# Two-layer encoder trunk on one core: rows of x and of the output moved one residue class per DMA, on two queues

## The chip, the cores and the metric

One core of one Trainium2 chip runs the whole program. The metric is device time in microseconds (us) of one execution, from the first to the last instruction. A program of this length is measured over several runs, and the median is compared.

## The reference, cut to what matters

```python
D_MODEL, SEQ, DEPTH, D_FF = 2048, 256, 2, 5632

def hybrid_layer(x, rel_bias, w_in, sink, w_pa, w_pb, w_out, ln1_g, ln1_b, w_up, w_down, ln2_g, ln2_b):
    proj = jnp.einsum('bsd,dc->bsc', x, w_in)                      # 10240 columns
    qa, ka, va, qb, kb, vb, ga, gb = jnp.split(proj, split_points, axis=-1)
    ya = dilated_mixture(qa, ka, va, rel_bias) @ w_pa              # dilations 1, 4, 16
    yb = windowed_gqa(qb, kb, vb, rel_bias, sink) @ w_pb
    merged = jax.nn.sigmoid(ga) * ya + jax.nn.sigmoid(gb) * yb
    x = layer_norm(DEEPNORM_ALPHA * x + merged @ w_out, ln1_g, ln1_b)
    gate, up = jnp.split(x @ w_up, 2, axis=-1)
    return layer_norm(DEEPNORM_ALPHA * x + (jax.nn.silu(gate) * up) @ w_down, ln2_g, ln2_b)

def reference(x, ...):                                             # x: (1, 256, 2048) float32
    for l in range(DEPTH):
        x = hybrid_layer(x, ...)
    return x
```

x and the output are 2.10 MB each (256 rows of 8 KB); the weights of both layers, all float32, are some 500 MB.

## The kernel before, in words

**Tokens.** The 256 tokens are kept in an order of residue classes: the rows 4q + a, q = 0 to 63, of class a (0 to 3) stand together. So a tile of 128 partitions holds two classes: half t = 0 has classes 0 and 1, half t = 1 classes 2 and 3. The residual stream lies in four tiles res[c] (c = 0 to 3), each [128 partitions, 2 halves, 512 columns]. token_rows (lines 70 to 73) describes in DRAM the rows of one half t: two classes of 64 rows each, 4 rows apart, 512 columns (2 KB) of each row. load_x(c) (lines 308 to 310) loads column chunk c of x by two DMAs, one for each half; leave (lines 786 to 789) multiplies, adds and stores one chunk of one half.

**Weights.** All products stream their weights in pieces of 512 KB (128 partitions of 1024 float32). load_to (line 118) issues a piece's DMA on SP's queue into one of six raw buffers; split_to makes two exact parts of it, the high one on ACT (line 128, whi) and the low one on DVE (line 129, wlo). Each product is three matmuls (lines 215 to 217 with the activations stationary, 171 and 202 with the weights stationary). run (lines 137 to 152) goes through the pieces in program order; splits are issued three pieces ahead of the products (fewer for the first two pieces), loads five further, as far as the six raw buffers are free. Every engine and every queue executes in the order in which the code issues.

**Start.** busy(n) issues n matmuls of zeros on PE (line 316). Then come the loads of x and of the first weights on SP, then make(0) and make(1). make(i) transposes two 128-column tiles of x with the identity on PE (line 369, four matmuls), copies the result as the high part on ACT (line 290) and takes the low part on DVE (line 291); the tile is called xT. make(2) to make(7) run just ahead of pieces 0 to 5 of the first product; chunk c of x serves make(2c) and make(2c + 1). Piece j of the first product needs tile xT j. The first product (group 0 of va) has 8 pieces of two row tiles of w_in, each with 12 matmuls of 512 columns (two row tiles, two halves of the tokens, three products); its result is taken off PSUM by ACT at line 290 (va<-acc). Ahead of piece 6 setup_small issues 15 small loads on SP (lines 324 to 335).

**Just after the start.** The bias table ftab is written to DRAM by 7 DMAs of 640 KB on SP (line 351), one after each of seven pieces, so these writes and weight loads take turns in SP's queue.

**End.** The last layer norm works on half t = 0, then on t = 1; for each, DVE alternates centre (line 784) and leave (line 788) over the four chunks, and SP issues a store after each leave (line 789).

Of the kernel before, what the change touches and what calls it, by code (L numbers as in the profile page):

```python
# [17 lines left out]
D_MODEL = 2048  # L18
SEQ = 256
# [27 lines left out]
def bias_tables():  # L47
    """Over the offsets key - query, in the order [residue difference][quotient difference]: one-hot rows
    (group, bucket), and what masks the offsets out of a head's reach; both depend on shapes alone."""
    half = NUM_BUCKETS // 2  # L50
    exact = half // 2
    delta = np.arange(-3, 4)[:, None]
    step = np.arange(-63, 65)[None, :]
    d = 4 * step + delta
    n = np.abs(d)
    scaled = np.log(np.maximum(n, 1) / exact) / math.log(MAX_DISTANCE / exact)
    large = np.minimum(exact + (scaled * (half - exact)).astype(np.int64), half - 1)
    bucket = np.where(d > 0, half, 0) + np.where(n < exact, n, large)
    keep = [(d % dil == 0) & (n <= (win // (2 * dil)) * dil) for win, dil in A_GROUPS]
    keep.append(n <= B_HALF)  # L60
    hot = np.zeros((4, NUM_BUCKETS, 7, P), np.float32)
    mask = np.zeros((N_HEADS, 7, P), np.float32)
    for g, ok in enumerate(keep):
        for b in range(NUM_BUCKETS):
            hot[g, b] = ok & (bucket == b)
        mask[A_HG * g:(A_HG * (g + 1) if g < 3 else N_HEADS)] = np.where(ok, 0.0, NEG)
    return hot.reshape(4 * NUM_BUCKETS, 7 * P), mask.reshape(N_HEADS, 7 * P)


def token_rows(dram, t, c0, width):  # L70
    """Rows of a (SEQ, D_MODEL) array in the kernel's order: position 64 * (i % 4) + i // 4."""
    return bass.AP(tensor=dram.tensor, offset=dram.offset + 2 * t * D_MODEL + c0,
                   ap=[[D_MODEL, 2], [4 * D_MODEL, 64], [1, width]])


@with_exitstack
def trunk(ctx: ExitStack, tc: tile.TileContext, x, rel_bias, w_in, sink, w_pa, w_pb, w_out,
          ln1_g, ln1_b, w_up, w_down, ln2_g, ln2_b, hot, mask, eye, out):
    nc = tc.nc
# [23 lines left out]

# [1 line left out]
    pieces = []  # L105
# [31 lines left out]
    def run():  # L137
        """Splits run ahead of the products, further ahead where a layer norm follows."""
        for m, pc in enumerate(pieces):
            ahead = min(AHEAD_SPLIT, 1 + m)  # L140
            for n in norms:
                if n - 24 <= m < n:
                    ahead = max(ahead, min(n - m + AHEAD_NORM, AHEAD_SPLIT + (m - n + 24) // 3))
            split_to(m + 1 + ahead)
            if pc["pre"]:
                pc["pre"]()
            pc["mm"](pc)
            if pc["post"]:
                pc["post"]()
            if background:  # L150
                background.pop(0)()
            pieces[m] = None
# [4 lines left out]
    def gemm_w(w, c0, xs, post, pre=None, turn=None):  # L157
        """out^T (256 columns of w from c0, tokens): weights stationary. With turn, the products with the
        high parts of the first half of the tokens come before turn(), which makes the second half."""
        kts = w.shape[0] // P  # L160
# [58 lines left out]
    def gemm_a(w, k0, k1, c0, width, xs, post, pre=None, turn=None):  # L219
        """out (tokens, width columns of w from c0) over the row tiles k0:k1: activations stationary. With  # L220
        turn, some products with the first half of the tokens come before turn(), which makes the second."""
        kk = 1024 // width
# [27 lines left out]
    def gemm_a_halves(w, k0, k1, c0, width, xs, post, between):  # L250
        """As gemm_a, with the first half of the tokens done before the second is begun."""
        kk = 1024 // width
# [40 lines left out]
    def triple(out, a, b, start, stop):  # L293
        """out (+)= a^T b by the parts (high, low) of both."""
        nc.tensor.matmul(out, lhsT=a[0], rhs=b[0], start=start, stop=False)  # L295
        nc.tensor.matmul(out, lhsT=a[0], rhs=b[1], start=False, stop=False)  # L296
        nc.tensor.matmul(out, lhsT=a[1], rhs=b[0], start=False, stop=stop)  # L297

# [1 line left out]
    res = [const.tile([P, 2, 512], F32, name=f"res{c}") for c in range(4)]  # L300
# [7 lines left out]
    def load_x(c):  # L308
        for t in range(2):
            nc.sync.dma_start(res[c][:, t, :], token_rows(x, t, c * 512, 512))  # L310

    def busy(n):
        """Keeps the tensor engine's clock up where it waits for operands."""
        ps = acc_tile()
        for _ in range(n):
            nc.tensor.matmul(ps[:, 0, 0:256], lhsT=zeros[:, 0:P], rhs=zeros, start=True, stop=True)
# [38 lines left out]
    def load_bias(dst, head, t, a0, na):  # L355
        """dst (128 queries of half t, na * 64 keys): bias by key - query, masked where out of reach."""
        for e in range(2):
# [4 lines left out]

# [1 line left out]
    def turn_rows(i):  # L364
# [28 lines left out]

# [1 line left out]
    def ln_scale(stats, t):  # L395
# [31 lines left out]
    def residual_gemm(w, k0, k1, xs, scale, stats, after, between, pre=None):  # L427
        """res = scale * res + (xs @ w); with stats, their statistics too, then after(t) for each half."""
        def update(c, t, c0, width, acc):
# [26 lines left out]
    def ln_turned(stats, vec, g, b):  # L456
        """A layer norm on the way to the next products. after(t) follows the last column of a half of the
        tokens; between() turns most of the first half; turn() the second, once products with the first are
        under way; late() the rest of both."""
        tiles = []  # L460
# [46 lines left out]

# [1 line left out]
    def soft_a(st, s, t, pair, qk):  # L509
        """Joint softmax over the three groups' keys for one head slot and half of the queries."""  # L510
        ps = aux_tile()
# [123 lines left out]

# [1 line left out]
    def layer(l, xt, pre, turn, after_last):  # L637
# [18 lines left out]
        def put(dst, acc, scale=None):  # L656
            """dst = scale * the product; with no dst, its two parts in a new tile."""
            tmp = evac_tmp(acc, 1.0 if scale is None else scale)
# [111 lines left out]

# [1 line left out]
    def turned(stats):  # L772
# [5 lines left out]
    def final(stats):  # L778
        def after(t):
# [6 lines left out]
            def leave(c):  # L786
                r = res[c][:, t, :]
                nc.vector.scalar_tensor_tensor(r, r, rstd, gbs[c][:, 1, :], op0=ALU.mult, op1=ALU.add)
                nc.sync.dma_start(token_rows(out, t, c * 512, 512), r)
            centre(0)  # L790
# [17 lines left out]
    nc.gpsimd.memset(minus_half, -0.5)  # L808
    busy(18)
    load_x(0)  # L810
    nc.sync.dma_start(ident, eye)
    for c in range(1, 4):
        load_to(c)
        load_x(c)
    make(0)
    split_to(1)
    make(1)
    busy(8)
    run()


# [26 lines left out]
```

## Time and profile before

| | us |
|---|---|
| median of 3 runs | 2867.54 |
| lowest and highest run | 2866.95, 2868.29 |
| span of the profiled execution | 2867.3 |
| PE busy in it | 2785.0 (97%) |
| DVE, ACT busy in it | 1592.0, 1263.0 |

The span is the time from the first to the last instruction of the profiled execution; no other time is given for that execution, and its span lies inside the range of the runs, 0.2 us under their median. PE is busy nearly everywhere, so the places where it is not are what the slices and windows of the trace have to show. A DMA's row on a queue (SPq) is the time that issuing it took, not the time in which its bytes moved; that is read from the DMA columns of the windows view.

### The profile page before, as it was taken

The numbers are of one execution on the slowest core, as the hardware profiler recorded it, in microseconds if no ns is written. First come the engines' busy times: TensorE is split into PE (matmuls) and PEld (weight loads), VectorE is DVE, ScalarE is ACT, GpSimd is POOL, SyncE is SP. The second block draws the span as 40 slices with busy tenths as digits, with TensorE's granted clock in tenths as the row PEclk, the third lists the DMA queues.
The fourth block names the chain that finished last, engine by engine and source line by source line (L and its number), as shares of the span: only waits on it lengthen the run. The fifth ranks groups of instructions, "written<-read, shape, count | busy, mean of one in ns | idle before, by whom it ended". The sixth has DMA issues, their size and how long they took to land.

```text
span 2867.3 us, 38494 instructions
## 1 busy us (share of the span) xinstructions
PE 2785.0 (97%) x15463; PEld 2414.2 (84%) x15463; DVE 1592.0 (56%) x1886; ACT 1263.0 (44%) x1600; POOL 5.4 (0%) x13
## 2 busy tenths in 40 slices
PE   5999999999999999999999999999999999999994
PEld 4788888888888888888888888888888888888884
DVE  2466555666655545555666655656675555455543
ACT  2344454454444533444344544445454444344440
POOL 0000000000000000000000000000000000000000
PEclk8999999999999999999999999999999999999997
DMA  4766556565665655655746666556756556565561
GB/s 141 222 198 177 181 184 191 184 197 167 210 192 191 206 176 183 193 182 191 236 148 198 183 179 188 181 186 187 234 155 193 188 177 210 180 194 180 183 232 48
DMA packets 494502, 532.07 MB, mean 186 GB/s; under 512 B 51808, under 2 KB 423520, under 8 KB 494324
## 3 DMA queue, kind: packets, MB, share of 16 engines
q1 hardware_dynamic: 494324, 529.62, 58.5%
q8 instruction: 121, 1.98, 0.3%
q14 instruction: 57, 0.47, 0.1%
HBM read 522.86 MB, written 6.68 MB: 185 GB/s over the span
## 4 chain that ended last, share of the span: by engine, by line
PE 94%; SPq 2%; DVE 1%; DMA 1%; ACT 0%; issue 0%; DVEq 0%; POOL 0%; ACTq 0%; POOLq 0%
PE acc L202 43%; PE acc L171 22%; PE acc L216 9%; PE acc L215 9%; PE acc L217 9%; DMA raw<-in_w_in_dram 1%; SPq L118 1%; SPq L310 1%; PE aux L297 0%; PE aux L296 0%; PE aux L295 0%; DVE xT L391 0%; PE aux L550 0%; PE aux L516 0%; PE aux L608 0%; PE aux L532 0%
## 5 line engine op out<-in xcount | busy, mean ns | idle before, releaser
L202 PE MATMUL acc<-xT,whi 128*128 128x512 f32 x4880 | 1719.5, 398 | 0.0
L171 PE MATMUL acc<-xT,wlo 128*128 128x256 f32 x4928 | 1357.2, 281 | 0.0
L129 DVE TENSOR_TENSOR wlo<-raw,whi 128x1024 fp32r<-128x1024 f32 x960 | 1126.6, 1221 | 271.4 <-ACT whi L128 266.7
L128 ACT ACTIVATE whi<-raw 128x1024 fp32r<-128x1024 f32 x960 | 965.4, 1050 | 356.0 <-DMA raw<-in_w_down_dram 125.8
L202 PEld LDWEIGHTS acc<-xT,whi 128*128 128x128 f32 x4880 | 909.0, 188 | 205.9 <-DVE xT L391 0.3
L171 PEld LDWEIGHTS acc<-xT,wlo 128*128 128x128 f32 x4928 | 931.2, 189 | 13.4
L281 ACT ACTIVATE tmp<-acc 128x512 f32<-128x512 f32 x186 | 110.9, 596 | 744.8 <-PE acc L202 744.5
L215 PE MATMUL acc<-whi,hT 128*128 128x512 f32 (+1 forms) x784 | 288.1, 367 | 0.0
L217 PE MATMUL acc<-whi,hT 128*128 128x512 f32 (+1 forms) x784 | 288.1, 367 | 0.0
L216 PE MATMUL acc<-wlo,hT 128*128 128x512 f32 (+1 forms) x784 | 288.1, 367 | 0.0
L666 DVE TENSOR_TENSOR sg<-acc,tmp 128x512 f32<-128x512 f32 x76 | 52.5, 691 | 242.1 <-ACT tmp L281 242.1
L216 PEld LDWEIGHTS acc<-wlo,hT 128*128 128x128 f32 x784 | 147.8, 189 | 24.5
L215 PEld LDWEIGHTS acc<-whi,hT 128*128 128x128 f32 x784 | 147.8, 189 | 24.4
L217 PEld LDWEIGHTS acc<-whi,hT 128*128 128x128 f32 x784 | 147.8, 189 | 24.2
L753 DVE TENSOR_TENSOR tmp<-acc,tmp 128x512 f32<-128x512 f32 x44 | 30.4, 692 | 178.0 <-ACT tmp L281 178.0
L215 PE MATMUL acc<-whi,mT 128*128 128x512 f32 (+1 forms) x320 | 111.1, 347 | 0.0
L215 PE MATMUL acc<-whi,xT 128*128 128x512 f32 (+1 forms) x256 | 97.8, 382 | 13.6 <-ACT xT L290 9.1
L216 PE MATMUL acc<-wlo,mT 128*128 128x512 f32 (+1 forms) x320 | 110.9, 347 | 0.0
L217 PE MATMUL acc<-whi,mT 128*128 128x512 f32 (+1 forms) x320 | 110.9, 347 | 0.0
L434 DVE SCALAR_TENSOR_TENSOR res<-res,acc 128x1024 f32<-128x1024 f32 (+2 forms) x20 | 20.2, 1008 | 153.1 <-PE acc L217 153.1
L216 PE MATMUL acc<-wlo,xT 128*128 128x512 f32 (+1 forms) x256 | 96.9, 378 | 2.7 <-DVE wlo L129 2.7
L217 PE MATMUL acc<-whi,xT 128*128 128x512 f32 (+1 forms) x256 | 96.6, 377 | 0.0
(137 smaller groups left out, 1632.5 us busy)
## 6 DMA issues: line engine op xcount, KB each, us to landing
raw<-in_w_up_dram SPq DMA_DIRECT2D x352, 512.0 KB
raw<-in_w_in_dram SPq DMA_DIRECT2D x320, 512.0 KB
raw<-in_w_down_dram SPq DMA_DIRECT2D x176, 512.0 KB
raw<-in_w_out_dram SPq DMA_DIRECT2D x64, 512.0 KB
raw<-in_w_pb_dram SPq DMA_DIRECT2D x32, 512.0 KB
raw<-in_w_pa_dram SPq DMA_DIRECT2D x16, 512.0 KB
bias<-ftab SPq DMA_DIRECT2D x96, 64.0 KB
ftab<-fb SPq DMA_DIRECT2D x7, 640.0 KB
```

The costliest lines, as they stand in the source:

```text
L118: nc.sync.dma_start(pc["raw"], pc["src"])
L128: nc.scalar.activation(hi, raw, AF.Copy)
L129: nc.vector.tensor_tensor(out=lo, in0=raw, in1=hi.bitcast(F32), op=ALU.subtract)
L171: nc.tensor.matmul(st["acc"][:, n, 0:SEQ], lhsT=lo[:, k, n * P:(n + 1) * P], rhs=xs(4 * j + k)[:, 0, :], start=False, stop=False)
L202: nc.tensor.matmul(acc, lhsT=hi[:, k, n * P:(n + 1) * P], rhs=xs(kt).rearrange("p h t -> p (h t)"), start=first and not turn, stop=last)
L215: nc.tensor.matmul(o, lhsT=xk[:, 0, ts], rhs=hi, start=first, stop=False)
L216: nc.tensor.matmul(o, lhsT=xk[:, 0, ts], rhs=lo, start=False, stop=False)
L217: nc.tensor.matmul(o, lhsT=xk[:, 1, ts], rhs=hi, start=False, stop=last)
L281: nc.scalar.activation(tmp, acc[:, :, SEQ:2 * SEQ], AF.Copy, scale=scale)
L310: nc.sync.dma_start(res[c][:, t, :], token_rows(x, t, c * 512, 512))
L666: nc.vector.tensor_tensor(out=dst, in0=acc[:, :, 0:SEQ], in1=tmp, op=ALU.add)
L753: nc.vector.tensor_tensor(out=tmp, in0=acc[:, :, 0:SEQ], in1=tmp, op=ALU.add)
```

## The change

A load or store of one half (two classes, 128 rows) becomes two DMAs of one class (64 rows, 64 partitions) each. Classes 0 and 2 (partitions 0 to 63 of either half) go on SP's queue as before, classes 1 and 3 (partitions 64 to 127) on ACT's queue, for x and for the output. The number of DMAs doubles, 8 to 16 each; the bytes are the same. At the start, the identity is loaded ahead of x; one weight piece stands between chunks 0 and 1 of x, two between 1 and 2 and two between 2 and 3, in place of one each. The 18 matmuls of zeros ahead of the first transposes become 30; the 8 after make(1) are gone. Docstrings and comments are also removed, so line numbers shift by 1 to 3.

```diff
-def token_rows(dram, t, c0, width):
-    return bass.AP(tensor=dram.tensor, offset=dram.offset + 2 * t * D_MODEL + c0,
-                   ap=[[D_MODEL, 2], [4 * D_MODEL, 64], [1, width]])
+def token_rows(dram, a, c0, width):
+    return bass.AP(tensor=dram.tensor, offset=dram.offset + a * D_MODEL + c0,
+                   ap=[[4 * D_MODEL, 64], [1, width]])
...
     def load_x(c):
-        for t in range(2):
-            nc.sync.dma_start(res[c][:, t, :], token_rows(x, t, c * 512, 512))
+        for a in range(4):
+            queue = nc.sync if a % 2 == 0 else nc.scalar
+            queue.dma_start(res[c][64 * (a % 2):64 * (a % 2 + 1), a // 2, :], token_rows(x, a, c * 512, 512))
...
             def leave(c):
                 r = res[c][:, t, :]
                 nc.vector.scalar_tensor_tensor(r, r, rstd, gbs[c][:, 1, :], op0=ALU.mult, op1=ALU.add)
-                nc.sync.dma_start(token_rows(out, t, c * 512, 512), r)
+                for e in range(2):
+                    queue = nc.sync if e == 0 else nc.scalar
+                    queue.dma_start(token_rows(out, 2 * t + e, c * 512, 512), r[64 * e:64 * (e + 1)])
...
-    busy(18)
+    busy(30)
+    nc.sync.dma_start(ident, eye)
     load_x(0)
-    nc.sync.dma_start(ident, eye)
     for c in range(1, 4):
-        load_to(c)
+        load_to(2 * c - 1)
         load_x(c)
     make(0)
     split_to(1)
     make(1)
-    busy(8)
     run()
```

SP's queue at the start of the program, before (ident is the identity, raw a weight piece, res_77 to res_80 the chunks 0 to 3 of x):

```order
L310 DMA res_77<-in_x_dram 128x1x512 x2
L811 DMA ident<-const_eye_dram 128x128
L118 DMA raw<-in_w_in_dram 128x2x512
L310 DMA res_78<-in_x_dram 128x1x512 x2
L118 DMA raw<-in_w_in_dram 128x2x512
L310 DMA res_79<-in_x_dram 128x1x512 x2
L118 DMA raw<-in_w_in_dram 128x2x512
L310 DMA res_80<-in_x_dram 128x1x512 x2
L118 DMA raw<-in_w_in_dram 128x2x512 x12
```

Each of these eight loads of x has 128 rows; three weight pieces stand ahead of the last chunk. The same queue at the same place with the change:

```order
L813 DMA ident<-const_eye_dram 128x128
L311 DMA res_77<-in_x_dram 64x512 x2
L118 DMA raw<-in_w_in_dram 128x2x512
L311 DMA res_78<-in_x_dram 64x512 x2
L118 DMA raw<-in_w_in_dram 128x2x512 x2
L311 DMA res_79<-in_x_dram 64x512 x2
L118 DMA raw<-in_w_in_dram 128x2x512 x2
L311 DMA res_80<-in_x_dram 64x512 x2
L118 DMA raw<-in_w_in_dram 128x2x512 x10
```

SP still issues eight loads of x, each of 64 rows now; the identity is first, and five weight pieces stand ahead of the last chunk. ACT's instructions at the start of the program, as a difference:

```order
+L311 DMA res_77<-in_x_dram 64x512 x2
+L311 DMA res_78<-in_x_dram 64x512 x2
+L311 DMA res_79<-in_x_dram 64x512 x2
+L311 DMA res_80<-in_x_dram 64x512 x2
 L290 ACT_TABLE_LOAD
 L290 ACTIVATE xT<-aux 128x2x256
```

All eight of ACT's loads are issued ahead of its table load and of its first copy of a transposed tile. ACT's instructions at the end of the program with the change (the splits of line 128 are its last work before; SP has eight stores of the same form at its end):

```order
L128 ACTIVATE whi<-raw 128x1024 x37
L792 DMA out_dram<-res_77 64x512
L792 DMA out_dram<-res_78 64x512
L792 DMA out_dram<-res_79 64x512
L792 DMA out_dram<-res_80 64x512
L792 DMA out_dram<-res_77 64x512
L792 DMA out_dram<-res_78 64x512
L792 DMA out_dram<-res_79 64x512
L792 DMA out_dram<-res_80 64x512
```

Before, ACT ended with the splits, and SP's eight stores had the form 2x64x512.

## Rows read from the trace of the kernel before

**Rows 1.** Busy time by stage: window, length, PE, PEld, DVE, ACT, POOL; clock, DMA share, GB/s

```profile
0.00:73.50 73.50, 40.66 (x155) 30.61 (x156) 18.28 (x21) 16.36 (x20) 0.30 (x5) 0.81 0.44 138
73.50:150.00 76.50, 71.33 (x352) 59.65 (x351) 32.83 (x31) 27.17 (x28) 0.00 (x0) 0.96 0.82 238
150.00:2822.00 2672.00, 2668.69 (x14926) 2319.76 (x14925) 1530.46 (x1817) 1219.51 (x1552) 4.19 (x7) 1.00 0.59 188
2822.00:2867.30 45.30, 4.34 (x37) 4.13 (x35) 10.46 (x18) 0.00 (x0) 0.92 (x1) 0.59 0.12 46
```

**Rows 2.** The same view, stretches in which x or the output moves

```profile
2.00:3.00 1.00, 1.00 (x7) 0.69 (x6) 0.00 (x0) 0.01 (x1) 0.00 (x0) 1.00 0.12 4
20.00:25.00 5.00, 0.48 (x1) 0.18 (x1) 0.00 (x0) 0.00 (x0) 0.00 (x0) 0.57 0.13 51
...
2836.00:2864.00 28.00, 0.00 (x0) 0.00 (x0) 0.00 (x0) 0.00 (x0) 0.00 (x0) 0.50 0.13 51
2864.00:2867.30 3.30, 0.00 (x0) 0.00 (x0) 0.00 (x0) 0.00 (x0) 0.00 (x0) 0.50 0.08 32
```

**Rows 3.** The same view, stretches of other transfers, and one at the low clock

```profile
26.70:30.80 4.10, 4.10 (x12) 3.24 (x11) 1.83 (x2) 1.55 (x2) 0.00 (x0) 0.50 0.24 67
...
85.00:120.00 35.00, 35.00 (x160) 29.15 (x160) 10.93 (x10) 6.63 (x7) 0.00 (x0) 1.00 0.74 195
120.00:135.00 15.00, 10.22 (x65) 9.12 (x63) 3.94 (x4) 3.66 (x4) 0.00 (x0) 0.89 0.79 211
135.00:150.00 15.00, 14.61 (x82) 13.21 (x82) 9.39 (x9) 7.87 (x8) 0.00 (x0) 0.89 1.09 351
160.00:164.00 4.00, 4.00 (x25) 3.53 (x24) 0.69 (x1) 0.88 (x2) 0.00 (x0) 1.00 1.17 267
```

**Rows 4.** Longest waits in 0 to 74 us: who waited for what, us, times, longest

```profile
ACT whi L128 <- DMA raw<-in_w_in_dram: 34.0, 4, 13.3
...
PE aux L369 <- DMA res<-in_x_dram: 11.4, 3, 4.7
```

**Rows 5.** Timeline, start: start us, us, engine, line, operation, out<-in, [idle <-releaser]

```profile
0.73 1.28 ACT L290 ACT_TABLE_LOAD   x1 [0.73 <-PEq L832]
0.73 1.30 SPq L310 DMA_DIRECT2D res<-in_x_dram  x2
...
1.05 4.02 PE L316 MATMUL acc<-zeros 128*128 128x256 bf16 x18 [1.05 <-DVE zeros L807]
...
14.37 1.94 PE L369 MATMUL aux<-ident,res 128*128 128x128 f32 x8 [9.29 <-DMA ident<-const_eye_dram]
...
17.07 1.23 DVE L129 TENSOR_TENSOR wlo<-raw,whi 128x1024 fp32r<-128x1024 f32 x1 [0.25 <-ACT whi L128]
```

**Rows 6.** Chain of waits, 60 to 75 us: start us, us, what

```profile
64.84 0.44 PE aux L369 x4
65.28 0.23 PE acc L215
```

**Rows 7.** ACT's timeline, end of the first product

```profile
73.52 1.03 ACT L290 ACTIVATE va<-acc 128x1024 fp32r<-128x1024 f32 x1 [5.71 <-PE acc L217]
```

**Rows 8.** SP's issues by line: loads of x, then the bias loads of 64 rows: ns min/median/max

```profile
L310 SPq DMA_DIRECT2D res<-in_x_dram x8: 537/1236/5465, 0.7 to 30.8; - x8
L360 SPq DMA_DIRECT2D bias<-ftab x160: 573/607/1213, 158.2 to 1749.3; - x160
```

**Rows 9.** SP's timeline, the last small load and the next weights

```profile
73.14 0.37 SPq L335 DMA_DIRECT2D masks<-const_mask_dram  x1
73.61 10.40 SPq L118 DMA_DIRECT2D raw<-in_w_in_dram  x6
```

**Rows 10.** Timeline, end of the program

```profile
2822.59 28.49 SPq L789 DMA_DIRECT2D out_dram<-res  x8
...
2831.66 1.41 DVE L788 SCALAR_TENSOR_TENSOR res<-res,rstd,gb 128x512 f32<-128x512 f32 x2
```

## The prediction, made before the changed kernel was run

> **What bounds the kernel now.** I read the busy time by stage first. Between 150 and 2822 us PE is busy 2668.69 of 2672.00 us [rows 1]: no transfer can shorten that stretch. PE's idle time lies elsewhere: 32.8 us of the first 73.5, 5.2 of the next 76.5, and 41.0 of the last 45.3 [rows 1]. The change touches the first and the last of these.
>
> The DMA columns tell why. While x alone moves, and while the output moves, the 16 DMA engines are busy 0.13 on average and carry 51 GB/s [rows 2]. 2 of 16 is 0.125, so two engines do all the work at 25.5 GB/s each, and each of these DMAs has two classes of rows. 2.10 MB at 51 GB/s are 41 us, and there are two such transfers. Weight loads of 128 rows reach 1.09 and 351 GB/s [rows 3]. At the end the last multiply-add of DVE is over at 2833.07 us (2831.66 + 1.41), all engines stand still, and 34 us later the program ends [rows 10]. At the start the longest wait is not for x but for weights: ACT waits 34.0 us for pieces, PE 11.4 us for x directly [rows 4]. A piece is spread over all engines, so its share on the two slow ones queues behind x. The first product ends at 73.5 us, where ACT takes it over [rows 7].
>
> **The end of the program.** Removed: 8 stores on two engines. Added: 16 stores of 64 rows, 8 of them on ACT, which has no work left there. What a 64-row DMA does, the trace shows once: the bias loads have 64 rows outermost, and where they are issued in the tail of weight loads the DMA share is 1.17 and the rate 267 GB/s, though with runs of 256 bytes [rows 3]; issuing one takes 0.61 us [rows 8]. So I take all 16 engines and a rate between 267 and 351 GB/s. By then only the last chunk counts, since DVE hands over 256 KB for every two operations of 0.7 us [rows 10], below that rate: last multiply-add at 2833.07; about 1.3 us from the issue to the first byte, as at the start (issue at 0.73, first bytes just after 2 us [rows 2, 5]); 256 KB at 300 GB/s, 0.9 us; from the last byte to the end 1.2 us (0.08 of 16 engines in 3.3 us is 2.1 us of two engines, so the bytes end at 2866.1 of 2867.3 [rows 2]). The end falls at 2836.5, **30.8 us** earlier. Bounds: at 188 GB/s, the mean of the long middle stretch [rows 1], the second half's 1.05 MB take 5.6 us from 2831 on, the end is 2837.9 and the gain 29.4; with nothing at all for bytes it is 31.7.
>
> [...]
>
> **The start.** I build the time at which the first product ends.
> - *Zeros.* 18 matmuls take 4.02 us from 1.05 [rows 5]; 30 take 6.7 and end at 7.7. The transposes queue behind them on PE and start at about 7.6.
> - *x and the identity.* SP issues the identity, then two loads of chunk 0, at 0.65 each (1.30 for two [rows 5]): done at 2.7. ACT issues its two by then as well. First bytes 1.3 us after an issue, 0.58 MB at 300 GB/s (2 us), completion 1.2: at about 6 us chunk 0 is there. Hidden by the zeros, which are therefore the bound; without them this would be the bound 1.5 us earlier.
> - *ACT's eight issues.* 8 x 0.61 to 0.69 from 0.73 end at 6.2, the table load of 1.28 us [rows 5] at 7.5. ACT's first copy waits for the transposes until 8.7. Cost nothing, with 1 us to spare. Behind these issues on ACT are the copy, the first split, and through them DVE and PE. If an issue takes 1.24 us, the median of SP's on clogged engines [rows 8], the copy starts 3.3 us late; that is kept for the range.
> - *First piece.* Before, from the first transpose (14.37) to the end of the first low split (17.07 + 1.23) it took 3.9 us, with the piece in place [rows 5]. Now 7.6 + 3.9 = 11.5. The piece itself: ahead of it and with it go 0.06 + 0.5 + 0.5 MB and nearly 0.5 MB of ACT's queue, some 5 us at 300 GB/s from 2.1, landed at about 8.5, so hidden too.
> - *Eight pieces.* A matmul steps by 0.23 us [rows 6]; a piece has 12 (two row tiles, two halves, three products), so eight take 8 x 12 x 0.23 = 22.1. Five groups of four transposes stand between, 0.44 each [rows 6]: 2.2. Sum 11.5 + 24.3 = 35.8.
> - *Supply.* Weights and x together are 0.8 MB for each of the first pieces, 2.7 us at 300 GB/s, then 0.5 MB or 1.75 us, against 3.2 us of PE per piece with its transposes. ACT and DVE are busy 16.4 and 18.3 us of the first 73.5 [rows 1], which hold the work for these eight pieces and more: 2.3 us a piece at most. So PE is the bound once it is running.
> - *Clock.* [...] The zeros now reach to the transposes and only a gap of 1 to 3 us is left ahead of the first piece. I take 1 us, between 0 and 3.
>
> The first product ends at 36.8 in place of 73.5: **36.7 us** earlier. Bounds: without the clock loss and with zeros partly at the high clock 34.0, gain 39.5; with transfers at 188 GB/s [rows 1] (2.1 MB of x and 4.2 MB of pieces, 33.5 us, from 2.1, then split and product of the last piece, 5 us) 40.6; with ACT's issues 3.3 us late and 3 us lost to the clock 42.1, gain 31.4.
>
> **Is it kept?** After 73.5 the next stretch must simply move forward. In program order ACT cannot split further than piece 10 until it has taken the first product off [rows 7], and the loads go no further than six raw buffers ahead, so the lead of the weights at that point has the same upper limit. SP reaches the next weights at 73.61, after the small loads [rows 9], about when the product ends. Now the small loads start once the split of piece 8 is done, some 10 us before the product ends, and take the same 8 us: the same relation. The writes of ftab then take turns with weights, PE lives on its lead (it is busy all of 85 to 120) and then starves, 4.8 us of 120 to 135 [rows 3], with some low clock after it. That hole should move forward unchanged, 0 us in the sum, +3 to -2.
>
> **Sum.** 2867.3 - 36.7 - 30.8 = 2799.8 us against the span; the median of the runs is 0.2 above it, so **2800.0 us**. By the bounds above the forecast's own range is 2794 to 2810.
>
> **Rivals.**
> 1. *The hole behind the start grows.* If the weights have a smaller lead when the writes of ftab begin, the hole takes back part of the gain. Six raw pieces at 12 x 0.23 = 2.76 us are 16.6 us at most: up to 2816.6. For it: the DMA engines had a mean share of 0.44 in the first 73.5 us [rows 1] and must do the same work in half the time. Against it: 300 GB/s is 1.6 times what PE eats.
> 2. *ACT is held by its own queue.* If each of its eight issues takes the longest that SP's took, 5.47 us [rows 8], they end at 44.5, the table load at 45.8, and the product 28 us after that, at 74: nothing gained at the start, 2836.7. SP's long issues came with two engines clogged; with 16 in use that should not be.
> 3. *No gain in either place.* If 64-row transfers of one class each are as slow together as one of two classes (each on one engine, the two queues on different ones), 51 GB/s stay, and so does the time: 2867.5. [...]
> 4. *Slower.* If the number of engines follows the number of classes, a one-class DMA runs on one engine, and both queues on the same one: 25.5 GB/s in place of 51. 2.10 MB take 82 us, 41 more at each end: 2949. It decides as soon as the share in the x loads falls under 0.125. Against it: the bias loads, also of one class of 64 rows, beside 1.17.
>
> **How the numbers follow.** Forecast 0.80, rival 1 beyond the forecast's range 0.10, rival 2 0.05, rival 3 0.02, rival 4 0.03. The range 2794 to 2817 holds the forecast and rival 1. A measurement of this kernel tells 0.2% (6 us) from no change. Faster: forecast, rivals 1 and 2, 0.95; same: rival 3, 0.02; slower: rival 4, 0.03.
>
> **What would show it.** In the profile of the changed kernel: DMA shares near 1 and over 250 GB/s in 3 to 15 us, ACT's first split near 9 us, the va copy of the first product at 34 to 43, the starved stretch at 85 to 100 in place of 120 to 135, and the end some 3.5 us after DVE's last multiply-add. A share of 0.13 or 0.06 at either end, or a va copy beyond 45, would make the prediction wrong.

## The result, and the profile after

| | before | changed |
|---|---|---|
| median, us (runs) | 2867.39 (4) | 2805.52 (4) |
| lowest and highest run | 2866.95, 2868.29 | 2803.67, 2806.96 |
| profiled execution | span 2867.3 | 2805.18, span 2803.4 |
| first product handed to ACT at | 73.52 | 41.24 |
| program's end behind DVE's last multiply-add | 34.2 | 3.66 |

The ratio is 0.9782, with an interval of 0.9768 to 0.9797: faster by 2.2%, 61.9 us. The time forecast, 2800.0, lies 5.5 us under the median, and the range of 2794 to 2817 holds it. One run of the kernel before, beside experiment 7, took 2894.58 us at a mean granted clock of 0.926 where its other runs had 0.986 to 0.990; medians are compared throughout, and it does not move them.

Busy time by stage in the changed kernel, with the columns of [rows 1]: start to first product, the next stretch with the writes of ftab, the long middle, the end.

```profile
0.00:41.20 41.20, 34.90 (x159) 27.40 (x160) 18.13 (x21) 16.48 (x20) 0.30 (x5) 0.92 0.86 245
41.20:115.00 73.80, 68.38 (x345) 57.21 (x344) 32.95 (x31) 27.21 (x28) 0.00 (x0) 0.98 0.81 233
115.00:2790.00 2675.00, 2671.69 (x14945) 2322.42 (x14944) 1531.66 (x1819) 1219.54 (x1552) 4.20 (x7) 1.00 0.59 188
2790.00:2803.40 13.40, 3.01 (x26) 2.80 (x24) 9.13 (x16) 0.00 (x0) 0.92 (x1) 0.79 0.55 157
```

PE's idle time at the start fell from 32.8 us to 6.3 (41.20 - 34.90), and at the end from 41.0 to 10.4. In the second stage PE is still idle for 5.4 us (5.2 before), and the middle is full as it was.

**The end.** The stores stand on two queues now, and DVE's last two multiply-adds end at 2799.74 (2798.33 + 1.41). Three timeline rows answer to [rows 10], three windows to [rows 2]:

```profile
2796.45 3.78 SPq L792 DMA_DIRECT2D out_dram<-res  x4
2796.45 4.04 ACTq L792 DMA_DIRECT2D out_dram<-res  x4
2798.33 1.41 DVE L789 SCALAR_TENSOR_TENSOR res<-res,rstd,gb 128x512 f32<-128x512 f32 x2
```

```profile
2799.00:2800.00 1.00, 0.00 (x0) 0.00 (x0) 0.73 (x2) 0.00 (x0) 0.00 (x0) 0.50 0.88 240
2800.00:2801.00 1.00, 0.00 (x0) 0.00 (x0) 0.00 (x0) 0.00 (x0) 0.00 (x0) 0.50 0.74 178
2801.00:2802.00 1.00, 0.00 (x0) 0.00 (x0) 0.00 (x0) 0.00 (x0) 0.00 (x0) 0.50 0.97 344
```

The DMA share is 0.74 to 0.97 where it was 0.13, and the bytes are out by 2802.

**The start.** The longest waits of 0 to 45 us, against [rows 4], and ACT's timeline, against [rows 5, 7]:

```profile
DVE xT L291 <- ACT xT L290: 11.7, 1, 11.7
ACT L290 <- DMA res<-in_x_dram: 10.8, 1, 10.8
ACT whi L128 <- DMA raw<-in_w_in_dram: 7.8, 6, 2.8
```

```profile
0.73 10.02 ACTq L311 DMA_DIRECT2D res<-in_x_dram  x8
10.78 1.28 ACT L290 ACT_TABLE_LOAD   x1 [10.78 <-DMA res<-in_x_dram]
12.07 0.60 ACT L290 ACTIVATE xT<-aux 128x512 fp32r<-128x512 f32 x1
```

The wait for weights, 34.0 us before, is down to 7.8. In its place stands a new one: ACT's eight issues of x loads last from 0.73 to 10.75, and only behind them come the table load and the first copy, at 12.07. The transposes were done at 7.65 (6.61 + 1.04):

```profile
6.61 1.04 PE L370 MATMUL aux<-ident,res 128*128 128x128 f32 x8
```

An issue by itself is short. The view of one line gives ACT's and SP's eight (ns min/median/max):

```profile
L311 ACTq DMA_DIRECT2D res<-in_x_dram x8: 472/562/697, 0.7 to 10.3; - x8
L311 SPq DMA_DIRECT2D res<-in_x_dram x8: 465/480/596, 1.2 to 15.1; - x8
```

Eight times 0.56 us is 4.5 us of the 10; in the rest ACT's queue waited. The order of ACT's instructions, with their waits, shows for what. DMAHW0 and so on are eight counters that the DMAs of this program take in turn; the trace has each count as it comes.

```
L311 DMA res_77<-in_x_dram 64x512 x2
L311 DMA res_78<-in_x_dram 64x512 x2
L311 DMA res_79<-in_x_dram 64x512 [waits DMAHW0_49]
L311 DMA res_79<-in_x_dram 64x512 [waits DMAHW2_49]
L311 DMA res_80<-in_x_dram 64x512 [waits DMAHW4_49]
L311 DMA res_80<-in_x_dram 64x512 [waits DMAHW6_49]
L290 ACT_TABLE_LOAD
```

The loads of chunks 2 and 3 each wait for a DMA that stands eight DMAs earlier in the program and took the same counter. Counters 0, 2 and 4 belong to loads of chunk 0, counter 6 to the first weight piece. In the trace the count that a load waits for and its issue fall together: counter 0 has it at 3.61 us and the fifth issue begins at 3.63, counter 6 at 10.26 and the eighth at 10.28. The four waits are not alike: seven of the eight issues are over at 6.60 us (6.13 + 0.47), and the last begins at 10.28.

```profile
6.13 0.47 ACTq L311 DMA_DIRECT2D res<-in_x_dram  x1
10.28 0.47 ACTq L311 DMA_DIRECT2D res<-in_x_dram  x1
```

So ACT stood 3.7 us for the first weight piece, whose landing lets the last load of x go. An issue on ACT's own queue held up ACT.

**The DMA engines at the start,** again by windows:

```profile
8.00:10.00 2.00, 0.00 (x0) 0.00 (x0) 0.00 (x0) 0.00 (x0) 0.00 (x0) 1.00 1.08 209
14.20:17.60 3.40, 2.94 (x7) 2.15 (x7) 2.70 (x4) 1.54 (x2) 0.00 (x0) 0.50 1.06 223
17.60:19.00 1.40, 1.40 (x5) 1.05 (x4) 0.61 (x2) 1.06 (x1) 0.00 (x0) 0.50 1.04 351
20.00:22.20 2.20, 2.20 (x12) 1.82 (x11) 0.01 (x1) 0.65 (x1) 0.00 (x0) 1.00 1.05 200
24.00:28.00 4.00, 4.00 (x21) 3.31 (x20) 2.74 (x3) 1.94 (x3) 0.00 (x0) 1.00 1.05 383
```

The mean share is 1.04 or more in every one of them, all 16 engines' worth, so the change did what it says. But while loads of x and of weights take turns in the queues, the rate goes up and down between 200 and 351 GB/s; it is 383 in 24 to 28 us, once only weights move, into 128 partitions each. A full share is not a full rate.

**The hole behind the start** moved forward with the rest, to 85 to 100 us (PE idle 2.0 and 2.3 us in the second and third window), where [rows 3] had 4.8 us idle in 120 to 135:

```profile
85.00:90.00 5.00, 4.79 (x33) 4.30 (x31) 0.61 (x1) 1.06 (x1) 0.00 (x0) 1.00 0.67 192
90.00:95.00 5.00, 3.00 (x23) 2.80 (x23) 0.61 (x1) 0.00 (x0) 0.00 (x0) 1.00 0.72 189
95.00:100.00 5.00, 2.66 (x12) 2.46 (x13) 1.82 (x2) 1.54 (x2) 0.00 (x0) 0.79 0.78 196
```

Its idle time is nearly the same, but less time passed at the low clock: the second stage's mean is 0.98 where [rows 1] had 0.96.

**The accounts.** Span against span: first product 73.52 to 41.24, 32.3 us; from there to DVE's last multiply-add (2833.07 and 2799.74) 1.05 us; behind it 34.2 to 3.66, 30.6. The sum is 63.9, and 2867.3 - 2803.4 = 63.9.

### The profile page after: what moved, and what is told of

It is laid out like the page before. It is cut to its first block, busy times and chain, and to the rows that moved or that the text cites. A ratio compares the mean times of both kernels' runs of the same rounds, so it can differ in the third digit from the quotient of the medians.

```text
span 2803.4 us, 38529 instructions
## 1 busy us (share of the span) xinstructions
PE 2778.0 (99%) x15467; PEld 2409.8 (86%) x15467; DVE 1591.9 (57%) x1886; ACT 1263.2 (45%) x1600; POOL 5.4 (0%) x13
## 4 chain that ended last, share of the span: by engine, by line
PE 97%; DVE 1%; SPq 1%; DMA 1%; ACT 0%; issue 0%; DVEq 0%; POOL 0%; ACTq 0%; POOLq 0%
PE acc L202 44%; PE acc L171 22%; PE acc L216 9%; PE acc L217 9%; PE acc L215 9%; SPq L118 1%; PE aux L297 0%; PE aux L296 0%; PE aux L295 0%; DMA res<-in_x_dram 0%; DMA raw<-in_w_in_dram 0%; DVE xT L392 0%; PE aux L551 0%; PE aux L517 0%; PE aux L609 0%; PE aux L533 0%
```

## The experiments

Each ran beside the kernel before on the same chip; "va copy" is the time at which ACT takes the first product off in the profiled execution (41.24 in the changed kernel). It varies from execution to execution: three traces with the changed kernel's start have 40.51 to 41.24, three with the start of experiment 7 have 35.08 to 37.79.

**1. The two ends, one at a time.** The kernel before with the new stores alone, and the changed kernel with the old stores.

```diff
 before, stores only
-                nc.sync.dma_start(token_rows(out, t, c * 512, 512), r)
+                for e in range(2):
+                    queue = nc.sync if e == 0 else nc.scalar
+                    queue.dma_start(token_rows(out, 2 * t + e, c * 512, 512), r[64 * e:64 * (e + 1)])
```

> The kernel before with only the stores of the output changed (64 rows each, half of them on ACT's queue). Theory, 'outermost dimension': a DMA with two classes outermost runs on two engines, one with 64 rows outermost on all 16, and the two ends of the program add up independently. Then the end gains what the two traces show, from 34.2 us behind DVE's last multiply-add to 3.7: span 2836.7, time 2837 to 2839. Rival, 'shared gain': the end is short only because the start was moved too (other clock, other state of the queues): over 2845.

> The changed kernel with the stores of the kernel before (one half of two classes each, on SP). Theory 'outermost dimension': the first product ends at 41 us as with the whole change, the end takes 34 us again behind DVE's last multiply-add: span 2834, time 2834 to 2836. Rival 'shared gain': over 2840 or under 2825.

Stores alone: 2837.93 us (2837.09 to 2839.94, 4 runs), ratio 0.9895 [0.9881, 0.991]. Loads alone: 2834.85 (2832.65 to 2835.86, 4), ratio 0.9882 [0.9868, 0.9897]. Against the 2868.21 of before beside them the gains are 30.3 and 33.4 us, some 63.6 together, near the 61.9 of the whole: two separate gains, neither given back by the other. In the first the span ends 3.9 us behind DVE's last multiply-add, in the second 34.25 us behind it.

**2. One queue.** All DMAs of 64 rows on SP.

```diff
-            queue = nc.sync if a % 2 == 0 else nc.scalar
+            queue = nc.sync
...
-                    queue = nc.sync if e == 0 else nc.scalar
+                    queue = nc.sync
```

> The changed kernel with all its 64-row loads and stores on SP, none on ACT. Theory 'outermost dimension': one queue drives all 16 engines as well; ACT is free for its table load at once, so its first copy comes at 8 to 9 us in place of 12.07 unless chunk 0 of x is late; chunk 1 to 3 are issued later. Time 2800 to 2807. Rival, 'second queue': half or all of the gain comes from having two queues; DMA share in the x loads near 0.5 or under, time over 2815.

2805.42 us (2803.34 to 2808.26, 4), ratio 0.9782 [0.9767, 0.9796], the same as the changed kernel. The second queue brings nothing that shows in the time. In the profiled execution, the slowest of the four, ACT copies its first tile at 7.88 in place of 12.07, but the va copy stands at 41.02: a weight piece came late, ACT's next tile stood behind its split, and PE waited 1.94 us for that tile in 24 to 28 us.

```profile
24.00:28.00 4.00, 2.06 (x11) 1.47 (x9) 1.08 (x1) 2.17 (x3) 0.00 (x0) 0.94 1.05 386
```

**3. The outermost dimension alone.** The kernel before with rows taken in plain order: 128 rows are one dimension, everything else as before, one DMA for each half and all on SP. This kernel leaves out the order of residue classes, so it computes something else in the attention, with the same instructions.

```diff
-    return bass.AP(tensor=dram.tensor, offset=dram.offset + 2 * t * D_MODEL + c0,
-                   ap=[[D_MODEL, 2], [4 * D_MODEL, 64], [1, width]])
+    return bass.AP(tensor=dram.tensor, offset=dram.offset + P * t * D_MODEL + c0,
+                   ap=[[D_MODEL, P], [1, width]])
```

> The kernel before with only the access pattern of token_rows changed: half t is 128 consecutive rows, so that 128 rows stand outermost in one DMA on SP. The kernel then works on the tokens in their plain order, which is another computation in the attention, with the same instructions. Order of the start as before, 18 and 8 matmuls of zeros. Theory 'outermost dimension': DMA share in the x loads near 1, the end 4 us behind DVE's last multiply-add, time 2798 to 2812. Rival, 'halves': only splitting into two 64-row transfers spreads them: 2867. Rival, 'reordering': the gain at the start comes from the new order of loads and zeros; then the start gains little here, 2830 to 2837.

2799.56 us (2798.18 to 2801.32, 4), ratio 0.9763 [0.9746, 0.9779]. Neither halves, nor a second queue, nor a new order of the start is needed for the gain: it comes from the outermost dimension, 128 in place of 2. (The rows of one DMA also lie 8 KB apart here; the changed kernel, with 32 KB, shows that the gain does not need this.) The va copy stands at 34.78, 6.5 us ahead of the changed kernel, and x moves faster:

```profile
8.00:12.00 4.00, 2.37 (x12) 1.88 (x13) 1.82 (x2) 1.86 (x3) 0.00 (x0) 1.00 1.04 393
12.00:16.00 4.00, 4.00 (x21) 3.31 (x20) 2.71 (x3) 1.91 (x3) 0.00 (x0) 1.00 1.05 386
```

**4. What holds ACT.** The changed kernel, with chunks 2 and 3 on SP alone; ACT issues only the four loads that wait for no counter.

```diff
-            queue = nc.sync if a % 2 == 0 else nc.scalar
+            queue = nc.sync if a % 2 == 0 or c > 1 else nc.scalar
```

> The changed kernel, but ACT issues only its loads of chunks 0 and 1 of x; those of chunks 2 and 3 go on SP. In the changed kernel ACT's fifth to eighth load each wait until the DMA eight issues earlier has landed (eight completion counters in turn), so its table load comes at 10.78 us. Theory 'ACT held': that wait is what the start lacked; without it ACT's first copy comes at 8 to 9 us, the first product ends 3 us earlier (38), time 2801 to 2803.5. Rival 'supply': the pieces of the weights come too slowly while x is loaded, so that an earlier copy only waits for them: copy at 8 to 9, first product still at 40 to 42, time 2804 to 2808.

The wait is gone, in ACT's timeline; the last row is its first split, which stood at 12.57 in the changed kernel:

```profile
0.73 2.59 ACTq L311 DMA_DIRECT2D res<-in_x_dram  x4
3.35 1.28 ACT L290 ACT_TABLE_LOAD   x1 [3.35 <-issue]
7.12 0.60 ACT L290 ACTIVATE xT<-aux 128x512 fp32r<-128x512 f32 x1 [2.48 <-PE aux L370]
9.36 1.06 ACT L128 ACTIVATE whi<-raw 128x1024 fp32r<-128x1024 f32 x1 [1.65 <-DMA raw<-in_w_in_dram]
```

The first copy came 5 us sooner, but the split behind it now waits for its weight piece, and it is 3.2 us sooner. The va copy came at 37.95, 2.6 to 3.3 us ahead of the traces with the changed start. The median is 2803.6 (2803.02 to 2804.35, 4), ratio 0.9775 [0.9759, 0.9792]: 1.9 us lower, between the times that the theory and its rival gave, and too little to be told from the changed kernel. From va copy to the end of the span the profiled run took 2764.3 us where the changed kernel took 2762.2, so 2 of the 3.3 us were lost again behind the start. That ACT was held is shown; that the whole program took longer for it is not.

**5. Why x moves at 200 to 290 GB/s.** Two suspects: DMAs of 128 KB are too small, or rows 32 KB apart are slow to read. First, one DMA for both token halves, 256 KB into 64 partitions. Then, the changed kernel with 64 consecutive rows in each DMA, which like experiment 3 leaves out the order of residue classes.

```diff
 256 KB each
+            src = bass.AP(tensor=x.tensor, offset=x.offset + e * D_MODEL + c * 512,
+                          ap=[[4 * D_MODEL, 64], [2 * D_MODEL, 2], [1, 512]])
+            queue.dma_start(res[c][64 * e:64 * (e + 1)], src)
...
 consecutive rows
-    return bass.AP(tensor=dram.tensor, offset=dram.offset + a * D_MODEL + c0,
-                   ap=[[4 * D_MODEL, 64], [1, width]])
+    return bass.AP(tensor=dram.tensor, offset=dram.offset + 64 * a * D_MODEL + c0,
+                   ap=[[D_MODEL, 64], [1, width]])
```

> The changed kernel with x loaded by two DMAs per chunk in place of four: 64 partitions, both halves of the tokens (256 KB each), even partitions' half on SP, the other on ACT. No load of ACT waits for a counter any more. Theory 'ACT held': first copy at 8 to 9, first product at 37 to 39, time 2800 to 2803. Rival 'supply': the rows of a class lie 32 KB apart and move at the same low rate as now (200 to 290 GB/s at a DMA share of 1), first product at 39 to 42, time 2803 to 2807.

> The changed kernel with only the rows of a 64-row DMA changed: 64 consecutive rows (8 KB apart) in place of every fourth (32 KB apart). The kernel then works on the tokens in their plain order, another computation in the attention with the same instructions; ACT's eight loads and their waits stay. Theory 'row distance': rows 32 KB apart move slower on each DMA engine; now the rate in 8 to 20 us goes to 370 to 400 GB/s as in the run with 128 consecutive rows, first product at 36 to 39, time 2799 to 2803. Rival 'half partitions': transfers into 64 partitions are what is slow; rate stays 200 to 290 GB/s, time 2804 to 2807.

With 256 KB: 2801.95 us (2800.58 to 2803.83, 4), ratio 0.977 [0.9756, 0.9785], va copy at 36.22, the first copy at 7.40 since half as many DMAs stand in the queues; the rate in 8 to 20 us is still 275 to 304. With consecutive rows: 2805.71 (2804.29 to 2807.69, 4), ratio 0.9784 [0.9769, 0.9798], va copy at 40.58, and no higher rate while x moves:

```profile
8.00:12.00 4.00, 1.43 (x8) 0.93 (x8) 0.00 (x0) 1.02 (x1) 0.00 (x0) 0.86 1.03 240
20.00:24.00 4.00, 4.00 (x22) 3.28 (x21) 1.97 (x3) 2.51 (x3) 0.00 (x0) 1.00 1.05 239
```

The same two windows in the changed kernel:

```profile
8.00:12.00 4.00, 0.33 (x1) 0.14 (x1) 0.00 (x0) 1.22 (x1) 0.00 (x0) 1.00 1.07 225
20.00:24.00 4.00, 4.00 (x22) 3.32 (x21) 1.36 (x3) 2.21 (x3) 0.00 (x0) 1.00 1.05 271
```

Over the whole of 8 to 20 us the means are 255 GB/s in the changed kernel, 289 with 256 KB, 264 with consecutive rows, and 390 in experiment 3. The distance of the rows falls as a suspect, and the size explains a small part at most. What experiment 3 had and these have not is 128 partitions in one DMA.

**6. The order of the start.** The kernel with 256 KB loads, with the start of before: 18 and 8 matmuls of zeros, x ahead of the identity, one piece between chunks.

```diff
-    busy(30)
-    nc.sync.dma_start(ident, eye)
+    busy(18)
     load_x(0)
+    nc.sync.dma_start(ident, eye)
...
-        load_to(2 * c - 1)
+        load_to(c)
...
+    busy(8)
```

> As the run with both halves in one DMA, with the start of the kernel before: identity behind chunk 0, one weight piece between the chunks, 18 and 8 matmuls of zeros. Theory: the order of the loads and the number of zeros are worth little, since five pieces ahead of chunk 3 or three come to the same bytes before piece 4; time within 2 us of the run with both halves. Rival, 'the reordering is the gain': over 2808, with PE idle longer before the first piece and more of it at the low clock.

2807.9 us (2803.98 to 2808.98, 4), ratio 0.9788 [0.9774, 0.9803]: slower than the 2801.95 of the new order, and no run of either lies among those of the other. The va copy came at 39.83, 3.6 us later. By the va copies and the medians the new start is worth some 4 to 6 us with these loads; which of its parts (the order of the loads, the identity, the zeros) does it was not tested. I had thought it worth under 2; that was wrong.

**7. 128 partitions in one DMA, with the reference's rows.** Into partition 2q + e of a separate tile goes row 4q + 2t + e, so the outermost dimension is 64 and a DMA fills 128 partitions; the transposes put the tokens in order with a permuted identity. The residual's own rows are loaded much later (2.10 MB more). The start has the order and the zeros of the kernel before, and all loads of x are on SP.

```diff
+        for t in range(2):
+            nc.sync.dma_start(xin[c][:, t, :], bass.AP(tensor=x.tensor, offset=x.offset + 2 * t * D_MODEL + c * 512,
+                                                       ap=[[4 * D_MODEL, 64], [D_MODEL, 2], [1, 512]]))
...
+    nc.sync.dma_start(perm, bass.AP(tensor=eye.tensor, offset=eye.offset, ap=[[P, 64], [64 * P, 2], [1, P]]))
```

> The changed kernel once more, beside the next run on the same chip: 2803 to 2807, first product at 40 to 42.

> x for the first transposes is loaded by one DMA of 128 partitions for each half and chunk on SP, row 4q + a of the two classes in partition 2q + (a mod 2), so that 64 stands outermost in DRAM; the transposes use a matrix with permuted rows of the identity, which brings the tokens back into class order. The rows of x for the residual are loaded by 64-row DMAs on SP much later, in the middle of layer 0 (2.10 MB more traffic). Start in the order of the kernel before, 18 and 8 zeros; stores as in the changed kernel. Theory 'half partitions': only transfers into 64 partitions are slow, so the rate in 8 to 20 us is 370 to 400 GB/s though rows lie 8 and 24 KB apart, ACT's first copy comes at 6 to 7, the first product ends at 34 to 36, time 2798 to 2801; the later loads hide beside PE. Rival 'row distance': rate 200 to 290 GB/s, first product at 38 to 42, time 2803 to 2807. Rival 'traffic': the later loads of x delay weights in the middle, first product early but time over 2803.

The changed kernel again: 2805.66 us (2804.43 to 2806.77, 5). The wide copy: 2800.58 (2798.64 to 2803.09, 6), ratio to before 0.9756 [0.9727, 0.9785]. It beats both kernels, by 67 and by 5 us, so the later loads did not eat up the gain. The va copy stands at 37.21, where 34 to 36 was expected (35.08 in a second trace, in experiment 8). The rate reaches that of experiment 3 in 12 to 16 us, although the rows lie apart:

```profile
12.00:16.00 4.00, 4.00 (x15) 3.08 (x14) 1.86 (x3) 2.61 (x3) 0.00 (x0) 0.57 1.06 387
```

Over 8 to 20 us the mean is 361 GB/s, and 359 in the second trace, beside 289 for loads of the same 256 KB into 64 partitions. So the partitions of one DMA are what decides here: 359 to 390 GB/s on average while every DMA has 128, 232 (experiment 6) to 289 while loads into 64 take turns with weights, and down to 200 in parts of that (8 to 10 and 20 to 22.2 us above), at about the same share.

**8. The hole behind the start.** In the kernel of experiment 7 PE still stood idle for 5.7 us of 85 to 105, and ran at the low clock after it:

```profile
85.00:90.00 5.00, 1.95 (x14) 1.55 (x13) 1.23 (x1) 1.06 (x1) 0.00 (x0) 1.00 0.73 182
90.00:95.00 5.00, 2.56 (x19) 2.16 (x18) 1.49 (x2) 1.54 (x2) 0.00 (x0) 0.91 0.69 161
95.00:100.00 5.00, 5.00 (x24) 4.98 (x24) 1.11 (x2) 1.06 (x1) 0.00 (x0) 0.50 0.85 257
```

The seven writes of ftab are put behind every third piece in place of every one.

```diff
-            background.extend([lambda d=d: nc.sync.dma_start(
-                ftab[:, d], fb[:, d][:, None, :].to_broadcast([N_HEADS, 64, P])) for d in range(7)])
+            for d in range(7):
+                background.append(lambda d=d: nc.sync.dma_start(
+                    ftab[:, d], fb[:, d][:, None, :].to_broadcast([N_HEADS, 64, P])))
+                background.extend([lambda: None] * 2)
```

> The kernel with the wide copy once more, for the comparison on one chip. All theories: its median again, 2800.6 within 2 us, so 2798 to 2803, and some 5 us under the changed kernel's 2805.5.

> The kernel with the wide copy, with the seven writes of ftab spaced: one behind every third weight piece in place of one behind each. In the kernel without this, PE stood still for 5.7 us of 85 to 105 and ran at the half clock in part of it. Theory 'the hole is made by the writes taking turns with the weights, and it is what varies from run to run': with two pieces more between two writes PE has no idle time over 0.5 us between 70 and 130, the median falls by 5 to 9 us, to 2792 to 2796, and the runs lie within 2 us of each other. Rival 'the bytes have to be moved anyway': 4.6 MB of writes cost the weights' lead the same wherever they lie, the hole moves back or spreads over more pieces, and the median stays within 2 us, 2798 to 2803.

Beside the wide copy's 2802.14 us (2798.57 to 2804.24, 5; only 3.4 under the changed kernel's 2805.5 this time) this took 2792.75 (2790.99 to 2793.59, 4), ratio to before 0.9737 [0.9723, 0.975]: 9.4 us less, and the fastest kernel here, 75 us under before and 13 under the changed one. PE has no idle time left there:

```profile
70.00:90.00 20.00, 20.00 (x117) 17.74 (x116) 7.78 (x7) 5.96 (x7) 0.00 (x0) 1.00 0.85 255
90.00:110.00 20.00, 20.00 (x128) 18.00 (x127) 7.64 (x8) 7.53 (x10) 0.00 (x0) 1.00 0.88 272
```

With two more pieces between two writes the rate rose from 161 to 182 (85 to 95 us, with the hole) to 255 to 272 GB/s. The rival, that the bytes cost the same wherever they lie, falls. The gain lies behind the start: the va copy came at 37.79, no sooner than in the wide copy's traces, and from there to the end of the span it took 2754.0 us in place of 2763.2 and 2762.2. The runs spread over 2.6 us, not under 2 as I expected, against 5.7 beside them. That the hole is what varied from run to run is not shown. The wide copy's two traces (experiment 7 and this one) had nearly the same hole, 5.7 and 5.2 us of idle time:

```profile
40.00:130.00 90.00, 84.28 (x434) 71.33 (x433) 39.45 (x39) 31.45 (x35) 0.00 (x0) 0.96 0.79 222
40.00:130.00 90.00, 84.77 (x446) 71.72 (x445) 39.49 (x45) 31.64 (x38) 0.00 (x0) 0.98 0.82 232
```

Of the 3.1 us between their spans (2800.4 and 2797.3) 2.1 lie ahead of the va copy and 1.0 behind it.

## Why the prediction was right, and where it was off

**The bound.** Right. Two engines for x and for the output were the cause at both ends [rows 2], and experiment 3 removes both by the access pattern alone.

**The end.** Right: 30.8 us predicted, 30.6 measured; 3.66 us behind DVE where 3.4 were taken.

**The start.** Right in its mechanism, 36.7 us predicted and 32.3 measured. By its steps:
- *Zeros and x.* The transposes began at 6.61, not 7.6: 30 matmuls took 5.72 us, and x was there. This us was not gained, since ACT was not ready for them.
- *ACT's eight issues.* This step failed. The issue was sized well (0.56 us against 0.61 to 0.69), but "cost nothing, with 1 us to spare" overlooked that the last four wait for DMAs in flight, and the last of them for the first weight piece, 3.7 us. The first copy came at 12.07 and not 8.7, 3.4 us late. The text kept an end of 3.3 us for slow issues; the size agrees by chance, the cause was another one. The order of the changed kernel with its waits would have shown it.
- *First piece.* The forecast had it landed at about 8.5, hidden. The start of ACT's last issue puts its landing at about 10.2, and in experiment 4, with ACT free, the split still waited for it until 9.36. So with ACT free and the loads as they are the first split could have begun at about 10.2 at the earliest, not at the 9.2 or so of the forecast. By this estimate about 1 us of the 3.4 belongs to the piece, and the rest to ACT's queue.
- *Clock.* PE stood still from 7.65 to 12.62 but for one transpose, and was then granted 0.50 up to about 19 us. From the end of the first low split (14.87) to the va copy it took 26.4 us, where 24.3 and 1 for the clock were forecast. No run shows that 1 us, which was an estimate. What the run showed in its place: the window of that stretch has no idle time of PE and a mean clock of 0.91, 9% of 26.27 us; by this estimate 2.4 us went to the clock where 1 was taken, and that covers the remaining 1.1.

```profile
14.93:41.20 26.27, 26.27 (x116) 21.56 (x117) 15.99 (x18) 13.17 (x16) 0.00 (x0) 0.91 0.86 258
```

- *Supply.* 300 GB/s was too much while x moved (255 on average in 8 to 20 us), but PE did not wait for it: it is busy throughout from 14.93 us on. The conclusion stood, the rate did not; in experiment 2, with the copy 4 us earlier, the rate did show, as 1.94 us of PE's idle time.

**The hole.** Predicted 0, +3 to -2; measured -1.05.

**Around the span.** The sum took 0.2 us from the span to the median. In the runs beside the experiments, of every kernel and of before too, the time stood 1.74 to 1.88 us above the span; here it is 1.78. So the profiled execution of before, with its span of 2867.3, was a run some 1.7 us above the median.

Together: +4.4 (start) + 0.2 (end) - 1.05 (hole) + 1.6 (around) gives 2805.2, the profiled execution's 2805.18.

**The rivals.** 1, a growing hole, did not come: it moved, with its idle time nearly the same, and the stretch around it took 1.05 us less. 2, ACT held by its own queue, was the right place with a price ten times too high: the forecast had 36.7 us for it, and the first copy was 3.4 us late; experiment 4 shows the hold, and 2.6 to 3.3 us of it at the va copy. 3 and 4 needed a share of 0.13 or less; it was 1.05. Of the signs that the prediction named, one failed: the first split came at 12.57, not near 9.

**Halves of the partitions.** Moving x and the output in halves of 64 partitions gained 61.9 us, but a single transfer over 128 partitions is what beat the change once it was on 16 engines: 2799.56 us in experiment 3 and 2800.58 in experiment 7, beside 2805.52 and 2805.66. In the slow stretches above, loads into halves mixed with weights moved at 200 to 223 GB/s, well under my 300; the stores had 344 in 2801 to 2802.

## What to carry to other kernels

Look at the DMA share of a slow transfer first: 0.13 is 2 of 16 engines, and the cure here was an outermost dimension of 64 or 128, with rows 8 KB or 32 KB apart. Then look at GB/s beside a full share; loads into 64 partitions kept the share full at 232 to 289 GB/s on average where 128 had 359 to 390, so fill 128 in one. Be wary of loads on the queue of an engine that has work to start: here they held ACT's first copy up by 3.4 us, though what that cost in the end could not be told from noise. Space large writes out among a weight stream that has only a small lead: in experiment 8 it took 9.4 us off the median.

## What was not expected of the hardware

- The DMA share says little of the rate: 1.05 goes with 200 GB/s while loads of 64 partitions move, and with 383 while all have 128.
- An issue of 0.56 us can stand in its queue until an earlier DMA has landed, the last of ACT's for 3.7 us: eight issues took 10 us in place of 4.5.
- A short hole cost more than its idle time: 5.2 to 5.7 us of idle PE in the wide copy's two traces, in the one of experiment 7 with a stretch at the clock of 0.50 behind it (95 to 100 us), were worth 9.4 us in the median when removed.
